# Soft-routed experts by two levels of Strassen-Winograd: weight tiles on ScalarE's queue, and the weight sums in other places

## The chip, the cores and the metric

The kernel runs on one core of one Trainium2 chip. The metric is the device time of one execution in microseconds (us). A core has TensorE (PE, matrix products), VectorE (DVE, elementwise), ScalarE (ACT, here mostly copies), GpSimd (POOL) and SyncE (SP). DMAs are issued here from the instruction streams of SyncE and GpSimd, in their order, and carried by 16 DMA engines that all share.

## The reference

```
x: (16, 512, 512) f32    router_logits: (16, 512, 8) f32    expert_weights: (8, 512, 2048) f32
probs = softmax(router_logits)
output = sum over e of probs[:, :, e:e+1] * matmul(x, expert_weights[e])     # (16, 512, 2048) f32
```

With the probabilities multiplied into x, this is one product of an 8192 x 4096 matrix (tokens by experts times hidden) with a 4096 x 2048 matrix (the weights).

## The kernel before, in words

The large product is split in two along each of its three dimensions. Tokens are taken in 16 pairs q of blocks of 256 (2q and 2q + 1). The depth is split into experts 0 to 3 and 4 to 7, the columns into 0 to 1023 and 1024 to 2047. So the weights have four blocks, B11, B12, B21 and B22 (first digit: experts, second: columns). Strassen-Winograd needs seven products of sums of blocks, P1 to P7, instead of eight. Their right sides are B11 (P1), B21 (P2), T1 = B11 - B12 (P5), T2 = B22 + T1 (P6), T3 = B22 - B12 (P7), T4 = B21 - T2 (P4) and B22 (P3).

Each right side has four sub-blocks kn = (k, n), in f16 tiles of 128 x (8 x 512), 1 MB each (k: a pair of experts, n: 512 columns). A second level of the same scheme multiplies them in seven steps, in the order 1, 5, 6, 2, 7, 3, 4. Steps 1, 2 and 3 use the raw sub-blocks (0,0), (1,0) and (1,1); steps 5, 6, 7 and 4 use sums of them ("inner sums"), made by VectorE. So each right side is seven 1 MB tiles. The pool `wpool` has 15 tiles: a right side in use is seven, and the next one is built beside it.

One step is eight matmuls (128 x 512 output) and is called a slot: 8 x 0.216 = 1.73 us. A stage runs the seven steps of one or two products in turn, so a two-product stage has 14 slots, 24.17 us. The stages:

| stages | products | starts at (us) |
|---|---|---|
| 0 to 3 | P1, two q each | 42.2 |
| 4 to 9 | P2 and P1 | 147.8 |
| 10 to 14 | P2 alone, two q each | 292.9 |
| 15 (`k5`), 16 | P5 of q = 0 and 1; P6 of q = 0 (seven slots) | 419.9 |
| 17 to 30 | P6 and P5 | 456.3 |
| 31 (`k7`) | P6 and P7 | 797.1 |
| 32 to 46 | P4 and P7 | 829.5 |
| 47 (`k3`) | P4 and P3 | 1193.1 |
| 48 to 54, 55 | P3, two q each; the last P3 (seven slots) | 1228.6 |

What surrounds the steps:

- The left side of a step is x times a probability (`times`, z tiles), with differences; VectorE makes it one stage ahead. x comes as a block of 256 tokens: either cast to f16 by GpSimd's DMA into `xs` and turned by two DMA transposes on SyncE's queue (L393, `xT<-xs`), or loaded already turned (`xT<-x`). `start_loads(stage + 2)` is issued after slot 0 of a stage, `finish_loads(stage + 2)` (the transposes) after slot 6. There are 10 x tiles.
- After a step its PSUM bank is evacuated (`post`). A product that adds to an earlier one (P2, P6, P4) does it on VectorE (`h<-ps,h`, `ps<-ps,h`), with one copy on ScalarE (L532). A product that stands alone (P1, P5, P7, P3) has five ScalarE copies (L514, L518, L521) and two VectorE additions. The addend is an `h` tile that SyncE loads one stage ahead (`h<-kept`, `h<-out_dram`); results leave as `out_dram<-h` on GpSimd's queue. There are 12 h tiles and 8 PSUM banks. The bank of step 1 is written again by step 6, three slots after step 1 ends in a two-product stage.
- `at(stage, slot, f)` runs f just before that slot in program order. Every DMA and every VectorE and ScalarE instruction of the main part is pinned to its engine's program order. `later(cost, make)` queues VectorE work; a planner (`slack`, `need`) puts it between evacuations by its estimated cost, first in, first out; 2.29 is its cost of a whole-tile sum, 0.69 of a quarter.

The weights before the change:

- `cast_block(q, kn)` casts one sub-block from f32 (two GpSimd DMAs of 512 KB). `fetch_w` loads a stored f16 tile on SyncE's queue. `kept_w` names the copy in DRAM.
- `wedge` makes half a sub-block of T3, T1 and T2 and stores them. The wedges of (0,1) run in stages 0 and 1, and with them T4 of (0,1) in stage 2 (`early_t4`); those of the other three sub-blocks run in stages 4 to 9.
- P7's inner sums are made from four whole T3 tiles in stages 10 and 11 and stored. T1 and T2 are fetched in stages 12 and 13, P5's inner sums are made in stage 14, P6's in stage 15.
- T4 of the other three sub-blocks is made in stages 17 to 20 (`t4_at`). P4's inner sums are made by quarters (two of a tile's eight chunks at a time, all four sub-blocks in one tile) in stages 21 to 26, P3's in stages 35 to 44 (`sums_by_parts`).
- `turnover(stage, place, r, raw)` brings in the seven tiles of the next right side, one in two slots, as the tiles of the old one come free: for P7 in stages 29 and 30, for P4 in 30 and 31, for P3 in 45 and 46. P3's three raw tiles are cast anew from the f32 weights.

Of the kernel before, what the change touches and what calls it, by code (L numbers as in the profile page):

```python
# [31 lines left out]
def kernel(  # L32
# [125 lines left out]

    def fetch_w(what, kn):
        t = new_w()  # L160
        sp(t, stored[what, kn])
        return t

    def inner_sums(b, t7=None):
# [579 lines left out]
    def wedge(kn, e):  # L744

        t = new_w()
        a, b = t[:, ds(0, C), :], t[:, ds(C, C), :]
        rows = ds(e * C, C)

        def casts():  # L750
            cast_w(12, kn, e, a)
            cast_w(22, kn, e, b)

        def send(what, u):
            pool(kept_w(what, kn)[:, rows, :], u)

        def t3():
            u = new_u().rearrange("p (c two) t -> p c (two t)", two=2)
            tt(u, b, a, SUB)
            send("t3", u)  # L760

        def t1():
            tt(a, b11[kn][:, rows, :], a, SUB)
            send("t1", a)

        def t2():
            if kn == (0, 1):
                tt(b11[kn][:, rows, :], b, a, ADD)
                send("t2", b11[kn][:, rows, :])
            else:  # L770
                tt(b, b, a, ADD)
                send("t2", b)
        return casts, [t3, t1, t2]

    def wedge_at(stage, slot, kn, e, then):
# [15 lines left out]
    def cast21(kn):  # L791
        b21[kn] = cast_block(21, kn)

    def early_t4():
        kn = 0, 1

        def make():
            t = new_w()
            tt(t, b21[kn], b11[kn], SUB)
            pool(kept_w("t4", kn), t)  # L800
        later(2.29, make)

    wedge_at(0, 4, (0, 1), 0, (0, 13))
    at(0, 11, lambda: cast21((0, 1)))
    wedge_at(1, 2, (0, 1), 1, (1, 11))
    at(1, 8, lambda: cast21((0, 0)))
    at(2, 2, early_t4)
    at(2, 3, lambda: cast21((1, 1)))
    at(2, 10, lambda: cast21((1, 0)))

    def sums_at(stage, slot, r, of, ps):
        def go():
# [12 lines left out]
    def fetch_at_w(stage, slot, of, what, kn):  # L825
        at(stage, slot, lambda: of.__setitem__(kn, fetch_w(what, kn)))
    ORDER = ((0, 0), (0, 1), (1, 1), (1, 0))


    def sums_in_place(part, b, r, cost):  # L830

# [7 lines left out]
        one(6, b[1, 1], b[1, 1], b[0, 0])  # L839
        one(4, b[1, 0], b[1, 0], b[1, 1])  # L840

    def whole_sums(r, b):
        sums_in_place(lambda p, o: pool(kept_w((r, p), (0, 0)), o), b, r, 2.29)

    for i, kn in enumerate(ORDER):
        fetch_at_w(10, 1 + 3 * i, t3, "t3", kn)
        fetch_at_w(12, 1 + 3 * i, t1, "t1", kn)
        fetch_at_w(13, 1 + 3 * i, t2, "t2", kn)
    at(11, 2, lambda: whole_sums(7, t3))
    last2 = k5 - 1  # L850
    sums_at(last2, 4, 5, t1, (5,))
    sums_at(last2, 6, 5, t1, (6, 7))
    sums_at(last2, 8, 5, t1, (4,))
    sums_at(k5, 3, 6, t2, (5, 6))
    sums_at(k5, 8, 6, t2, (7, 4))


    def slots_after(stage, slot, n):
# [3 lines left out]
            stage += 1  # L862
        return stage, slot

    def t4_at(stage, slot, kn):
        t = []

        def make():
            tt(t[0], t[0], t2[kn], SUB)
            pool(kept_w("t4", kn), t.pop())  # L870
        at(stage, slot, lambda: t.append(cast_block(21, kn)))
        at(*slots_after(stage, slot, 11), lambda: later(2.29, make))

    def sums_by_parts(stage, slot, every, r, load):

        for j in range(4):
            b, chunks = {}, ds(2 * j, 2)

            def begin(b=b, j=j, chunks=chunks):
                t = new_w()  # L880
                for i, kn in enumerate(ORDER):
                    b[kn] = t[:, ds(2 * i, 2), :]
                    load(b[kn], kn, j, chunks)

            def go_on(b=b, chunks=chunks):
                sums_in_place(lambda p, o: pool(kept_w((r, p), (0, 0))[:, chunks, :], o), b, r, 0.69)
            at(*slots_after(stage, slot, j * every), begin)
            at(*slots_after(stage, slot, j * every + 8), go_on)

    def cast_part(t, kn, j, chunks):  # L890
        k, n = kn
        pool(t, expert_weights[HE + 2 * k + j // 2, ds(j % 2 * 2 * P, 2 * P),
                               ds(NH + n * NB, NB)].rearrange("(c p) n -> p c n", p=P))

    for i, kn in enumerate(((0, 0), (1, 0), (1, 1))):
        t4_at(*slots_after(k5 + 2, 4, 20 * i), kn)
    sums_by_parts(*slots_after(k5 + 2, 4, 62), 20, 4,
                  lambda t, kn, j, chunks: sp(t, kept_w("t4", kn)[:, chunks, :]))
    sums_by_parts(k7 + 4, 4, 36, 3, cast_part)


    RAW = {1: (0, 0), 2: (1, 0), 3: (1, 1)}

    def turnover(stage, place, r, raw):
# [2 lines left out]

        def fetch(p):
            if p in RAW:
                right[r].w[p] = raw(RAW[p])  # L910
            else:
                right[r].w[p] = new_w()
                sp(right[r].w[p], kept_w((r, p), (0, 0)))
        at(stage - 1, 9, lambda: fetch(1))
        for i, p in enumerate(STEPS[1:]):
            at(stage, place + 2 * i + 1, lambda p=p: fetch(p))
    turnover(k7 - 1, 1, 7, lambda kn: fetch_w("t3", kn))
    turnover(k7, 0, 4, lambda kn: fetch_w("t4", kn))
    turnover(k3 - 1, 1, 3, lambda kn: cast_block(22, kn))


    finish = products[3, 15]
# [72 lines left out]
```

## Time and profile before

| | |
|---|---|
| median of 3 runs | 1416.78 us (1416.09 to 1418.22) |
| the profiled execution | 1416.24 us, of which the span from first to last instruction is 1414.4 |
| matmul spacing in an undisturbed stage | 0.216 us |
| DMA queue of GpSimd (q0, software_dynamic) | 179.87 MB, 52.7% of 16 engines |
| DMA queue of SyncE (q1, hardware_dynamic) | 159.13 MB, 36.2% |
| whole-tile sum on VectorE (`w<-w`, 128 x 4096 f16) | 2.284 us |
| quarter sum (128 x 1024 f16) | 0.684 us |
| 1 MB tile from DRAM (`w<-wd`) | 13.7 us to landing (median of 30) |
| 256 KB quarter from DRAM (`w<-wd`) | 5.6 us (median of 16) |
| cast of 512 KB, of 256 KB | 11.2 us, 7.5 us (medians) |

One execution was profiled. Durations of instructions are of that execution; a group's idle time is put down to the event that came last before it ended. "To landing" is the time from the issue of a DMA to its completion. Times in the text count from the span's start.

### The profile page before, as it was taken

The numbers are of one execution on the slowest core, as the hardware profiler recorded it, in microseconds if no ns is written. First come the engines' busy times: TensorE is split into PE (matmuls) and PEld (weight loads), VectorE is DVE, ScalarE is ACT, GpSimd is POOL, SyncE is SP. The second block draws the span as 40 slices with busy tenths as digits, with TensorE's granted clock in tenths as the row PEclk, the third lists the DMA queues.
The fourth block names the chain that finished last, engine by engine and source line by source line (L and its number), as shares of the span: only waits on it lengthen the run. The fifth ranks groups of instructions, "written<-read, shape, count | busy, mean of one in ns | idle before, by whom it ended". The sixth has DMA issues, their size and how long they took to land.

```text
span 1414.4 us, 17403 instructions
## 1 busy us (share of the span) xinstructions
PE 1377.9 (97%) x6390; PEld 624.0 (44%) x6390; DVE 1105.4 (78%) x1271; ACT 183.8 (13%) x318; POOL 383.8 (27%) x600
## 2 busy tenths in 40 slices
PE   8998999999989999999999899999999999899998
PEld 4443444444434444444444344444444444344444
DVE  4956767669679888887877688888888986798882
ACT  2221111100001111111111000000000000122221
POOL 3233333321212232222211112232332333122231
PEclk9999999999999999999999999999999999999999
DMA  9999999998987989887975898888888889988786
GB/s 196 206 254 305 250 217 280 238 379 314 370 277 211 230 244 281 267 254 238 282 216 209 323 360 231 202 230 191 240 202 223 215 215 246 228 185 183 165 154 107
DMA packets 191893, 340.10 MB, mean 240 GB/s; under 512 B 52416, under 2 KB 87488, under 8 KB 186944
## 3 DMA queue, kind: packets, MB, share of 16 engines
q0 software_dynamic: 86576, 179.87, 52.7%
q1 hardware_dynamic: 105232, 159.13, 36.2%
q8 instruction: 50, 0.82, 0.2%
q14 instruction: 35, 0.29, 0.1%
HBM read 211.85 MB, written 155.39 MB: 260 GB/s over the span
## 4 chain that ended last, share of the span: by engine, by line
PE 81%; DMA 11%; DVE 3%; issue 2%; SPq 1%; POOL 1%; ACT 0%; DVEq 0%; POOLq 0%; ACTq 0%
PE ps L127 81%; DMA h<-kept 3%; DMA w<-in_expert_weights_dram 2%; DMA xT<-xs 2%; DMA out_dram<-h 2%; DMA h<-out_dram 1%; SPq L393 1%; DVE h L107 1%; DVE z L107 1%; DMA xs<-in_x_dram 1%; DMA xT<-x 1%; DMA w<-wd 1%; POOL w L121 0%; DVE w L107 0%; POOL out_dram L121 0%
## 5 line engine op out<-in xcount | busy, mean ns | idle before, releaser
L127 PE MATMUL ps<-w,z 128*128 128x512 f16 x5416 | 1182.6, 380 | 17.8 <-DVE h L107 15.4
L127 PEld LDWEIGHTS <-z 128*128 128x128 f16 x5416 | 530.6, 98 | 659.1 <-issue 23.3
L121 POOL DMA_DIRECT2D out_dram<-h x380 | 248.6, 679 | 838.0 <-ACT h L532 433.6
L107 DVE TENSOR_TENSOR h<-ps,h 128x512 f32<-128x512 f32 x415 | 281.8, 688 | 212.2 <-PE ps L127 184.2
L107 DVE TENSOR_TENSOR z<-xT,pT 128x2048 f16<-128x2048 f16 x220 | 267.1, 1218 | 21.3 <-DMA xT<-xs 14.8
L127 PE MATMUL ps<-w,d 128*128 128x512 f16 x880 | 203.1, 384 | 11.6 <-DVE ps L107 11.6
L127 PEld LDWEIGHTS <-d 128*128 128x128 f16 x880 | 87.1, 99 | 119.0 <-issue 17.9
L107 DVE TENSOR_TENSOR z<-z,d 128x2048 f16<-128x2048 f16 x110 | 132.6, 1217 | 0.0
L521 ACT COPY h<-ps 128x512 f32<-128x512 f32 x90 | 52.8, 587 | 389.2 <-PE ps L127 353.0
L532 ACT COPY h<-ps 128x512 f32<-128x512 f32 x64 | 37.6, 587 | 501.9 <-PE ps L127 499.6
L107 DVE TENSOR_TENSOR w<-w 128x1024 f16<-128x1024 f16 (+2 forms) x72 | 96.0, 1336 | 0.5
L107 DVE TENSOR_TENSOR z<-z,u 128x2048 f16<-128x2048 f16 x64 | 78.4, 1225 | 2.2
L107 DVE TENSOR_TENSOR u<-xT,pT 128x2048 f16<-128x2048 f16 x64 | 78.0, 1219 | 0.0
L107 DVE TENSOR_TENSOR d<-z 128x1024 f16<-128x1024 f16 x110 | 75.4, 686 | 2.6 <-PE ps L127 0.5
L518 ACT COPY h<-ps 128x512 f32<-128x512 f32 x90 | 52.9, 588 | 177.4 <-PE ps L127 167.7
L107 DVE TENSOR_TENSOR ps<-ps,h 128x512 f32<-128x512 f32 (+1 forms) x66 | 45.4, 689 | 26.4 <-PE ps L127 15.5
L121 POOL DMA_DIRECT2D w<-in_expert_weights_dram x61 | 46.1, 775 | 31.3 <-PE ps L127 11.6
L107 DVE TENSOR_TENSOR h<-h 128x512 f32<-128x512 f32 (+2 forms) x69 | 45.0, 675 | 11.7 <-DMA h<-kept 9.9
L121 POOL DMA_DIRECT2D kept<-h x56 | 30.7, 550 | 56.1 <-DVE h L107 19.6
L121 POOL DMA_DIRECT2D wd<-w x56 | 31.3, 559 | 39.3 <-DVE w L107 32.2
L514 ACT COPY ps<-ps 128x512 f32<-128x512 f32 x45 | 25.7, 571 | 117.3 <-PE ps L127 116.9
L107 DVE TENSOR_TENSOR z<-z 128x2048 f16<-128x2048 f16 x32 | 39.2, 1225 | 1.1
(45 smaller groups left out, 90.4 us busy)
## 6 DMA issues: line engine op xcount, KB each, us to landing
out_dram<-h POOLq DMA_DIRECT2D x380, 256.0 KB, 6.2
pT<-p_dram SPq DMA_DIRECT2D x140, 256.0 KB, 6.2
w<-wd SPq DMA_DIRECT2D x30, 1024.0 KB, 13.7
h<-kept SPq DMA_DIRECT2D x100, 256.0 KB, 5.7
xT<-x SPq DMA_DIRECT2D x87, 256.0 KB, 5.4
w<-in_expert_weights_dram POOLq DMA_DIRECT2D x43, 512.0 KB, 11.2
h<-out_dram SPq DMA_DIRECT2D x68, 256.0 KB, 5.6
kept<-h POOLq DMA_DIRECT2D x56, 256.0 KB, 6.8
```

The lines of the kernel that those rows point to most:

```text
L107: dve(nc.vector.tensor_tensor(out=o, in0=a, in1=b, op=op))
L121: note(nc.gpsimd.dma_start(out=o, in_=i, **how))
L127: note(nc.tensor.matmul(ps, z, w, start=start, stop=stop, skip_group_check=True))
L393: note(nc.sync.dma_start_transpose(out=self.t[:, :, ds(j * P, P)], in_=self.xs[:, j, :]))
L514: act(nc.scalar.copy(self.banks["b"], x))
L518: act(nc.scalar.copy(o[tn], q if p == 5 else x))
L521: act(nc.scalar.copy(o[TN[p]], b if p == 2 else x))
L532: act(nc.scalar.copy(o[tn], b))
```

## The change

1. `fetch_w` issues its DMA from ScalarE's stream instead of SyncE's. All three turnovers now use it, and they fetch one tile in three slots instead of two.
2. The wedges of (0,1) and `early_t4` go from stages 0 to 2. The four casts for P2's sums are placed ten slots apart. The T blocks of (0,1) (called `ODD`) are made from whole tiles in stages 10 to 15, from casts of all four blocks; T1 and T2 of (0,1) stay in SBUF, T3 and T4 are stored.
3. T1 of the other sub-blocks is fetched in stage 12, T2 in stage 14. P5's inner sums are made in stages 12 and 13, P6's in 14 and 15.
4. P7's inner sums are made by quarters in stages 17 to 20, from T3 quarters loaded on ScalarE's queue.
5. P4's quarters in stages 21 to 26 cast B21, subtract T2, store T4 and then make the inner sums; `t4_at` goes.
6. P3's quarters in stages 35 to 44 also store the raw B22 in f16, and the turnover to P3 fetches those tiles instead of casting.

The diff, cut to its core:

```diff
     def fetch_w(what, kn):
         t = new_w()
-        sp(t, stored[what, kn])
+        note(nc.scalar.dma_start(out=t, in_=stored[what, kn]))
         return t
     def inner_sums(b, t7=None):
...
             send("t1", a)
         def t2():
-            if kn == (0, 1):
-                tt(b11[kn][:, rows, :], b, a, ADD)
-                send("t2", b11[kn][:, rows, :])
-            else:
-                tt(b, b, a, ADD)
-                send("t2", b)
+            tt(b, b, a, ADD)
+            send("t2", b)
         return casts, [t3, t1, t2]
     def wedge_at(stage, slot, kn, e, then):
...
     def cast21(kn):
         b21[kn] = cast_block(21, kn)
-    def early_t4():
-        kn = 0, 1
-        def make():
-            t = new_w()
-            tt(t, b21[kn], b11[kn], SUB)
-            pool(kept_w("t4", kn), t)
-        later(2.29, make)
-    wedge_at(0, 4, (0, 1), 0, (0, 13))
-    at(0, 11, lambda: cast21((0, 1)))
-    wedge_at(1, 2, (0, 1), 1, (1, 11))
-    at(1, 8, lambda: cast21((0, 0)))
-    at(2, 2, early_t4)
-    at(2, 3, lambda: cast21((1, 1)))
-    at(2, 10, lambda: cast21((1, 0)))
+    for i, kn in enumerate(((0, 0), (0, 1), (1, 1), (1, 0))):
+        at(i * 10 // 14 + (i * 10 % 14 + 2) // 14, (i * 10 + 2) % 14, lambda kn=kn: cast21(kn))
     def sums_at(stage, slot, r, of, ps):
         def go():
...
     def fetch_at_w(stage, slot, of, what, kn):
         at(stage, slot, lambda: of.__setitem__(kn, fetch_w(what, kn)))
     ORDER = ((0, 0), (0, 1), (1, 1), (1, 0))
+    ODD = 0, 1
+    made = {}
+    def cast_odd(q):
+        made[q] = cast_block(q, ODD)
+    def odd_t():
+        def make1():
+            t1[ODD] = made[11]
+            tt(t1[ODD], made[11], made[12], SUB)
+        def make3():
+            tt(made[12], made[22], made[12], SUB)
+            pool(kept_w("t3", ODD), made.pop(12))
+        def make2():
+            t2[ODD] = made[22]
+            tt(t2[ODD], made[22], t1[ODD], ADD)
+        for make in (make1, make3, make2):
+            later(2.29, make)
+    def odd_t4():
+        def make():
+            tt(made[21], made[21], t2[ODD], SUB)
+            pool(kept_w("t4", ODD), made.pop(21))
+        later(2.29, make)
     def sums_in_place(part, b, r, cost):
...
         one(6, b[1, 1], b[1, 1], b[0, 0])
         one(4, b[1, 0], b[1, 0], b[1, 1])
-    def whole_sums(r, b):
-        sums_in_place(lambda p, o: pool(kept_w((r, p), (0, 0)), o), b, r, 2.29)
-    for i, kn in enumerate(ORDER):
-        fetch_at_w(10, 1 + 3 * i, t3, "t3", kn)
-        fetch_at_w(12, 1 + 3 * i, t1, "t1", kn)
-        fetch_at_w(13, 1 + 3 * i, t2, "t2", kn)
-    at(11, 2, lambda: whole_sums(7, t3))
     last2 = k5 - 1
-    sums_at(last2, 4, 5, t1, (5,))
-    sums_at(last2, 6, 5, t1, (6, 7))
-    sums_at(last2, 8, 5, t1, (4,))
-    sums_at(k5, 3, 6, t2, (5, 6))
-    sums_at(k5, 8, 6, t2, (7, 4))
+    for stage, slot, q in ((10, 1, 12), (10, 8, 22), (11, 1, 11)):
+        at(stage, slot, lambda q=q: cast_odd(q))
+    at(11, 10, odd_t)
+    for i, kn in enumerate(((0, 0), (1, 1), (1, 0))):
+        fetch_at_w(12, 1 + 4 * i, t1, "t1", kn)
+        fetch_at_w(last2, 2 + 2 * i, t2, "t2", kn)
+    sums_at(last2 - 2, 13, 5, t1, (5, 6))
+    sums_at(last2 - 1, 6, 5, t1, (7, 4))
+    at(last2, 8, lambda: cast_odd(21))
+    sums_at(last2, 11, 6, t2, (5, 6))
+    at(k5, 4, odd_t4)
+    sums_at(k5, 5, 6, t2, (7, 4))
     def slots_after(stage, slot, n):
...
             stage += 1
         return stage, slot
-    def t4_at(stage, slot, kn):
-        t = []
-        def make():
-            tt(t[0], t[0], t2[kn], SUB)
-            pool(kept_w("t4", kn), t.pop())
-        at(stage, slot, lambda: t.append(cast_block(21, kn)))
-        at(*slots_after(stage, slot, 11), lambda: later(2.29, make))
-    def sums_by_parts(stage, slot, every, r, load):
+    def part_of(what, kn, chunks):
+        return kept_w(what, kn)[:, chunks, :]
+    def by_parts(stage, slot, every, r, load, between, when):
         for j in range(4):
             b, chunks = {}, ds(2 * j, 2)
...
                     load(b[kn], kn, j, chunks)
             def go_on(b=b, chunks=chunks):
-                sums_in_place(lambda p, o: pool(kept_w((r, p), (0, 0))[:, chunks, :], o), b, r, 0.69)
+                for kn in b:
+                    if kn != ODD:
+                        between(b[kn], kn, chunks)
+            def end(b=b, chunks=chunks):
+                sums_in_place(lambda p, o: pool(part_of((r, p), (0, 0), chunks), o), b, r, 0.69)
             at(*slots_after(stage, slot, j * every), begin)
-            at(*slots_after(stage, slot, j * every + 8), go_on)
-    def cast_part(t, kn, j, chunks):
-        k, n = kn
-        pool(t, expert_weights[HE + 2 * k + j // 2, ds(j % 2 * 2 * P, 2 * P),
-                               ds(NH + n * NB, NB)].rearrange("(c p) n -> p c n", p=P))
-    for i, kn in enumerate(((0, 0), (1, 0), (1, 1))):
-        t4_at(*slots_after(k5 + 2, 4, 20 * i), kn)
-    sums_by_parts(*slots_after(k5 + 2, 4, 62), 20, 4,
-                  lambda t, kn, j, chunks: sp(t, kept_w("t4", kn)[:, chunks, :]))
-    sums_by_parts(k7 + 4, 4, 36, 3, cast_part)
+            if between is not None:
+                at(*slots_after(stage, slot, j * every + when[0]), go_on)
+            at(*slots_after(stage, slot, j * every + when[-1]), end)
+    def cast_part(q):
+        def load(t, kn, j, chunks):
+            k, n = kn
+            pool(t, expert_weights[(q // 10 - 1) * HE + 2 * k + j // 2, ds(j % 2 * 2 * P, 2 * P),
+                                   ds((q % 10 - 1) * NH + n * NB, NB)].rearrange("(c p) n -> p c n", p=P))
+        return load
+    def load_part(what):
+        def load(t, kn, j, chunks):
+            note(nc.scalar.dma_start(out=t, in_=part_of(what, kn, chunks)))
+        return load
+    def load_p4(t, kn, j, chunks):
+        (load_part("t4") if kn == ODD else cast_part(21))(t, kn, j, chunks)
+    def less_t2(t, kn, chunks):
+        def make():
+            tt(t, t, t2[kn][:, chunks, :], SUB)
+            pool(part_of("t4", kn, chunks), t)
+        later(0.69, make)
+    def keep_raw(t, kn, chunks):
+        pool(part_of("b22", kn, chunks), t)
+    by_parts(k5 + 2, 4, 14, 7, load_part("t3"), None, (7,))
+    by_parts(*slots_after(k5 + 2, 4, 58), 21, 4, load_p4, less_t2, (7, 13))
+    by_parts(k7 + 4, 4, 36, 3, cast_part(22), keep_raw, (9, 16))
     RAW = {1: (0, 0), 2: (1, 0), 3: (1, 1)}
...
         def fetch(p):
             if p in RAW:
-                right[r].w[p] = raw(RAW[p])
+                right[r].w[p] = fetch_w(raw, RAW[p])
             else:
-                right[r].w[p] = new_w()
-                sp(right[r].w[p], kept_w((r, p), (0, 0)))
+                right[r].w[p] = fetch_w((r, p), (0, 0))
         at(stage - 1, 9, lambda: fetch(1))
         for i, p in enumerate(STEPS[1:]):
-            at(stage, place + 2 * i + 1, lambda p=p: fetch(p))
-    turnover(k7 - 1, 1, 7, lambda kn: fetch_w("t3", kn))
-    turnover(k7, 0, 4, lambda kn: fetch_w("t4", kn))
-    turnover(k3 - 1, 1, 3, lambda kn: cast_block(22, kn))
+            at(*slots_after(stage, place + 1, 3 * i), lambda p=p: fetch(p))
+    turnover(k7 - 1, 1, 7, "t3")
+    turnover(k7, 0, 4, "t4")
+    turnover(k3 - 1, 1, 3, "b22")
     finish = products[3, 15]
```

## The prediction

> **What bounds the kernel now.** I read the page first, for the busiest engine; then the windows view by stage, for where that engine loses time; then the waits of TensorE, the timeline of VectorE in those stages, and the queue's own waits of SyncE with the DMA view, for what was late.
>
> ```profile
> span 1414.4 us, 17403 instructions
> PE 1377.9 (97%) x6390; PEld 624.0 (44%) x6390; DVE 1105.4 (78%) x1271; ACT 183.8 (13%) x318; POOL 383.8 (27%) x600
> ```
>
> TensorE is the bound, so only its idle time can be won. The windows view (columns: window, its length, busy time of each engine, granted clock, DMA share, GB/s) places it. The third row is an undisturbed two-product stage, 24.16 us; the others are stages 1, 2, 14, 17, 31, 32 and 47.
>
> ```profile
> 66.34:91.32 24.98, 24.33 (x113) 10.97 (x112) 13.85 (x14) 5.84 (x10) 10.05 (x16) 1.00 1.15 271
> 91.33:123.63 32.30, 25.99 (x113) 11.35 (x112) 20.27 (x20) 5.84 (x10) 10.27 (x17) 0.95 1.16 279
> 123.64:147.80 24.16, 24.16 (x113) 10.97 (x112) 17.68 (x16) 5.84 (x10) 6.66 (x12) 1.00 0.97 267
> 389.54:419.92 30.38, 26.01 (x113) 11.39 (x112) 21.51 (x23) 1.17 (x2) 3.26 (x7) 0.94 0.89 301
> 456.29:482.82 26.53, 24.34 (x113) 10.88 (x112) 22.73 (x28) 2.92 (x5) 6.62 (x11) 1.00 1.10 263
> 797.08:829.47 32.39, 26.68 (x113) 11.52 (x112) 22.00 (x27) 1.76 (x3) 4.32 (x9) 0.89 0.95 371
> 829.48:854.43 24.95, 24.32 (x113) 10.91 (x112) 20.34 (x24) 1.17 (x2) 5.40 (x9) 1.00 1.01 379
> 1193.07:1228.61 35.54, 26.99 (x113) 11.53 (x112) 21.74 (x24) 2.92 (x5) 7.10 (x9) 0.90 0.98 259
> ```
>
> The excess over 24.16 is 0.8 + 8.1 + 6.2 + 2.4 + 8.2 + 0.8 + 11.4 = 37.9 us; the waits view adds 0.8 us near the end: 38.7 us in all. Where the granted clock is under 1, matmuls ran at half speed after the stop, so a long stop costs more than its length (stage 2: 0.05 of 32.3 = 1.6 us more).
>
> Each long stop is VectorE late with a PSUM evacuation. The timeline (start, length, what, idle time before with its releaser) shows what held VectorE in stages 2, 14, 31 and 47:
>
> ```profile
> 112.67 1.22 DVE L107 TENSOR_TENSOR z<-xT,pT 128x2048 f16<-128x2048 f16 x1 [6.57 <-PE ps L127]
> ...
> 115.74 2.28 DVE L107 TENSOR_TENSOR w<-w 128x4096 f16<-128x4096 f16 x1
> 117.94 2.48 DVE L107 TENSOR_TENSOR h<-ps,h 128x512 f32<-128x512 f32 x4
> ```
>
> ```profile
> 400.23 0.70 DVE L107 TENSOR_TENSOR ps<-ps,h 128x512 f32<-128x512 f32 x1 [8.66 <-DMA h<-kept]
> ```
>
> ```profile
> 806.16 1.90 DVE L107 TENSOR_TENSOR h<-h 128x512 f32<-128x512 f32 x3 [9.92 <-DMA h<-kept]
> ```
>
> ```profile
> 1199.17 0.69 DVE L107 TENSOR_TENSOR h<-ps,h 128x512 f32<-128x512 f32 x1 [6.93 <-DMA h<-out_dram]
> ...
> 1215.02 0.69 DVE L107 TENSOR_TENSOR h<-ps,h 128x512 f32<-128x512 f32 x1 [7.56 <-DMA out_dram<-h]
> ```
>
> The first row names TensorE, but the last transpose into that xT landed at 112.48, the moment of release. So the losses come from DMAs that landed late, in stages full of weight traffic, plus one weight sum of 2.28 us in front of four evacuations.
>
> **The change, part by part.**
>
> *T blocks of (0,1) leave stages 0 to 2.* Removed there: four casts of 512 KB, six stores of 512 KB, one of 1 MB, and on VectorE 6 x 1.22 + 2.28 = 9.6 us; the four casts for P2's sums stay. The 2.28 us is the very row in front of the evacuations at 117.94. The transposes took 15.0 us (median) in stages 1 and 2, against 7.9 us in stages 5 to 8, which have one cast block and three half-MB stores a stage, no more than stages 1 and 2 keep. The last one, issued at 95.2, would land near 103 instead of 112.5, before VectorE asks at 106. I leave 1.5 us of the 9.0; bounds 0 and 6 (if transposes stay at 15 us, only the sum is gone).
>
> *They come back in stages 10 to 15:* three casts of 1 MB in stages 10 and 11 and one in 14, 3 x 2.28 + 2.28 us on VectorE, two stores. The fetch of four t3 tiles and the whole P7 sums leave 10 and 11, and t1 and t2 shrink from eight fetches to six. VectorE is busy 15.6 of 24.17 us in stage 10 (no weight sums), so 8.5 us a stage is free. From late in stage 11 to the end of 14 the T blocks (6.9), P5's sums (9.1) and half of P6's (4.6) make 20.6 us against 3.3 x 8.5 = 28. Before, all of P5's sums sat in stage 14.
>
> *Stage 14.* What was late there is h<-kept, issued at 389.7 for a slot that began at 379.2, because SyncE was held in four transposes from 376.7 to 389.0, between weight fetches of 12.4 us each. After, no weight fetch is issued in stage 13. Two transposes alone take 2.5 us of issue at 428.2, so four take 5 and the loads go out near 382; even at 10 us they land as they are asked for (391.5). I leave 0.5 of 6.2; bounds 0 and 5.
>
> *Stage 17.* TensorE waits 2.2 us there for a z that the planner makes behind an evacuation; nothing in stage 16 changes: 2.4 stays.
>
> *Turnovers to P7 and P4 (stages 30 to 32).* In stage 30 the small loads took 16.1 us (h<-kept) and 17.0 (h<-out_dram) behind 1 MB weight tiles in SyncE's queue, while out_dram<-h, on GpSimd's queue in the same window, took 8.0. With weights on ScalarE's queue I take 8 for the loads: issued at 783.4 to 790.0 they land by 798, and VectorE's wait of 9.92 ends 8 us sooner. Then the weights may be late instead. Thirteen tiles, 13.6 MB, are needed between slot 2 of stage 30 (776) and slot 12 of stage 32 (842 if nothing stops). Beside them runs the base traffic, 199 GB/s in stages 33 and 34: 13.1 MB in 66 us. At the 371 to 379 GB/s of stages 31 and 32, 26.7 MB take 71 us: 5 us late, less what is loaded ahead. I leave 3.5 of 9.0; bounds 0 and 9.
>
> *Turnover to P3 (46, 47).* Six casts of 512 KB leave GpSimd's queue. There out_dram<-h took 10.2 us (median; the one that freed the h at 1215 took 21.5), against 5.2 in stages 33 and 34; h<-out_dram took 11.5 behind four weight fetches. Now six fetches of 1 MB from 1172 on, one in 5.2 us, are 202 GB/s beside 199: slightly over the rate above, but the last tile has 17 us to land (ten slots) where 13.7 is the median. I leave 2.5 of 11.4; bounds 0 and 8. The three b22 tiles cost twelve more quarter stores in stages 35 to 44, where TensorE never waits.
>
> *Quarters in stages 17 to 27 and 35 to 44.* P7's sums: 16 x 0.68 = 10.9 us instead of 9.1; P4's twelve subtractions: 8.2 instead of 6.9. VectorE is busy about 20 us a stage there, and a quarter adds 2.7 to 4.8 in one to one and a half stages: hidden. A cast quarter lands in 7.5 us and is used after seven slots (12.1 us).
>
> *ScalarE's stream.* 27 tile fetches and 20 quarter loads at SyncE's 0.32 us are 15 us on an engine that idles 87%. But ScalarE works in order, and behind a waiting fetch stand the PSUM copies (L514, L518, L521). A copy of a two-product stage has three slots, 5.2 us, less its own 0.59: 4.6 us of slack. SyncE's waits show how long such a fetch may stand:
>
> ```profile
> SPq L118 <- DVE z L107: 448.1, 52, 23.5
> ...
> SPq L118 <- DMA w<-wd: 45.0, 19, 4.0
> ```
>
> The second kind (2.4 us on average) is the nearer one: a fetch waiting for an earlier DMA. It fits under 4.6. For this and for waits in stages that lose nothing today I add 1.0; bounds 0 (a gain is excluded: those stages lose nothing) and 8.
>
> **Sum.** Left: 1.5 + 0.5 + 2.4 + 3.5 + 2.5 + 0.8 + 1.0 = 12.2 of 38.7, a gain of 26.5 us. The profiled execution took 1416.2 us (span 1414.4 and 1.8 around it): 1389.7, and 1390.2 against the median of 1416.8, 0.5 above it. I say 1390.
>
> **Rivals.**
>
> *The loads stay late (0.20).* If what slowed them is the full set of DMA engines and not the order in one queue, a new queue wins nothing: stages 31 and 32 keep 9.0, 14 and 47 about half, 3 and 6; the gain is 7.5 + 3.2 + 5.4 - 1.0 = 15 us: 1402. For it: DMA shares of 0.95 to 1.16 in these stages. Against it: the 8.0 us beside 16.1 in one window. The Trainium skill says it outright (DMA: Bandwidth & Descriptors, "Issuing engines are not separate DMA queues"): DMAs of all issuing engines run on the same 16 engines and interleave, so that another issuer saves only the issue time; by that alone the move would be worth nothing and the time would be this rival's. The same page ("Queues, rings and completion order") has each engine take turns between the queues, which the 8.0 beside 16.1 agrees with.
>
> *New waits in the stages that took the work (0.12).* GpSimd's stores stand behind 1 MB casts in stages 10 and 11 as they did in 46 (10.2 us), h tiles return late, and a quarter's subtraction meets a cast that has not landed. Two stops of 4 to 5 us with their half-speed matmuls: 10 us more than forecast, 1400. Against it: stages 5 to 8 carry a cast block each and lose nothing.
>
> *ScalarE stuck (0.18), slower.* A fetch waits as SyncE's loads wait for a free x tile: 8.6 us on average (448.1 / 52), 23.5 at most. Each such wait ahead of a copy stops TensorE for 8.6 - 4.6 = 4.0 us, 5.6 with the half-speed matmuls. It turns the sign from five of the 27 fetches on (26.5 / 5.6); with eight the time is 1390 + 45 = 1435. For it: SyncE issues late in all three turnovers. Against it: fetches stand one slot or more after the last reader of a tile, and ScalarE issues none of the x loads.
>
> **Chances and range.** Forecast 0.50, loads late 0.20, new waits 0.12, ScalarE stuck 0.18. 0.2% (2.8 us) is about what a measurement here can tell from no change. The first three are faster; of the last, 0.02 is a near balance and 0.16 slower; faster 0.82. The range starts where all bounds are at zero, 1416.8 - 38.7 + 3.2 = 1381, and reaches past the second and third case to 1408 (six more than 1402, for their own spread), leaving the stuck case out.
>
> **What would show it.** Right: windows of stages 2, 14 and 47 near 24 to 27 us, 31 near 27, 17 still 26.5; h<-kept near 8 us in stage 30; no ACT copy waiting on a w<-wd. Wrong: ScalarE's copies late in stages 31, 46 and 47 with TensorE waiting for ACT (stuck), or h loads still at 16 us in stage 30 (late).

## The result

The changed kernel takes 1395.30 us (median of 4 runs, 1390.09 to 1396.55); beside it the kernel before took 1416.43 (4 runs, 1415.44 to 1418.22). The ratio is 0.9842, 95% interval 0.9814 to 0.9870. The forecast was 1390, so the direction and most of the size came out, with 5 us missing. The profiled execution of after took 1396.55 us, its slowest; that of before took 1416.24. In a later comparison one execution of the kernel before took 5199.72 us, a disturbed run that is left out of the ratio.

One correction first. The section on the kernel says that a product P7 stands alone and has five copies on ScalarE. It does not: it adds to an earlier product, is evacuated by VectorE, and has one copy (L532) on ScalarE. Only P1, P5 and P3 stand alone. So in stages 32 to 46 (P4 and P7), as in stages 10 to 14 (P2 alone), ScalarE has two copies a stage and, beside the DMAs it issues, nothing else. This matters below.

### The profile page after: what moved, and what is told of

The parts are those of the page before. It is cut to its first block, busy times and chain, and to the rows that moved or that the text cites. A ratio compares the mean times of both kernels' runs of the same rounds, so it can differ in the third digit from the quotient of the medians.

```text
span 1394.9 us, 17466 instructions
## 1 busy us (share of the span) xinstructions
PE 1373.0 (98%) x6390; PEld 621.7 (45%) x6390; DVE 1106.1 (79%) x1289; ACT 183.0 (13%) x318; POOL 400.8 (29%) x632
## 4 chain that ended last, share of the span: by engine, by line
PE 84%; DMA 6%; issue 5%; DVE 3%; POOL 2%; ACT 0%; SPq 0%; DVEq 0%; POOLq 0%; ACTq 0%
PE ps L127 84%; DMA out_dram<-h 2%; DMA wd<-w 1%; DMA h<-out_dram 1%; DVE z L107 1%; DVE h L107 1%; POOL out_dram L121 1%; DVE w L107 1%; DMA w<-in_expert_weights_dram 1%; POOL w L121 0%; DMA h<-kept 0%; POOL wd L121 0%; DVE ps L107 0%; POOL kept L121 0%; ACT h L326 0%
## 5 line engine op out<-in xcount | busy, mean ns | idle before, releaser
L107 DVE TENSOR_TENSOR w<-w 128x1024 f16<-128x1024 f16 (+2 forms) x92 | 100.8, 1102 | 7.9 <-DMA out_dram<-h 7.3
L532 ACT COPY h<-ps 128x512 f32<-128x512 f32 x64 | 37.5, 586 | 496.6 <-PE ps L127 478.7
L121 POOL DMA_DIRECT2D w<-in_expert_weights_dram x65 | 48.9, 793 | 51.6 <-DMA wd<-w 37.0
L121 POOL DMA_DIRECT2D wd<-w x86 | 48.3, 584 | 41.4 <-DVE w L107 36.9
L514 ACT COPY ps<-ps 128x512 f32<-128x512 f32 x45 | 25.7, 571 | 111.3 <-PE ps L127 110.9
## 6 DMA issues: line engine op xcount, KB each, us to landing
w<-in_expert_weights_dram POOLq DMA_DIRECT2D x35, 512.0 KB, 11.2
```

The costliest lines, as they stand in the source:

```text
L107: dve(nc.vector.tensor_tensor(out=o, in0=a, in1=b, op=op))
L121: note(nc.gpsimd.dma_start(out=o, in_=i, **how))
L514: act(nc.scalar.copy(self.banks["b"], x))
L532: act(nc.scalar.copy(o[tn], b))
```

## The profile after

From the page of the changed kernel: TensorE's busy time fell by 5 us (fewer half-speed matmuls), GpSimd's rose by 17, and a queue q10 is new: ScalarE's.

```profile
span 1394.9 us, 17466 instructions
PE 1373.0 (98%) x6390; PEld 621.7 (45%) x6390; DVE 1106.1 (79%) x1289; ACT 183.0 (13%) x318; POOL 400.8 (29%) x632
...
q10 hardware_dynamic: 6768, 33.56, 6.9%
```

The windows view of the changed kernel, with the columns as before: window, its length, busy time of PE, PEld, DVE, ACT and POOL, granted clock, DMA share, GB/s. The rows are stages 1, 2, 12, 14, 17, 26, 31, 32 and 47.

```profile
65.98:90.15 24.17, 24.17 (x113) 10.94 (x112) 12.48 (x14) 5.83 (x10) 8.68 (x14) 1.00 1.13 236
90.15:114.32 24.17, 24.17 (x113) 10.93 (x112) 11.09 (x13) 5.82 (x10) 6.59 (x11) 1.00 1.20 237
331.89:361.86 29.97, 26.17 (x113) 11.36 (x112) 24.98 (x27) 1.18 (x2) 6.47 (x12) 0.94 0.88 291
386.04:410.20 24.16, 24.16 (x113) 10.94 (x112) 20.29 (x23) 1.17 (x2) 5.88 (x11) 1.00 1.07 346
446.57:473.09 26.52, 24.33 (x113) 10.85 (x112) 23.94 (x30) 2.92 (x5) 7.20 (x13) 1.00 0.94 278
667.52:694.36 26.84, 24.32 (x113) 10.94 (x112) 22.14 (x29) 3.34 (x6) 11.06 (x20) 1.00 0.95 269
791.80:815.96 24.16, 24.16 (x113) 10.94 (x112) 21.31 (x26) 1.76 (x3) 4.30 (x9) 1.00 1.03 398
815.97:840.13 24.16, 24.16 (x113) 10.94 (x112) 20.44 (x24) 1.17 (x2) 5.35 (x9) 1.00 1.04 377
1178.57:1208.99 30.42, 26.02 (x113) 11.33 (x112) 21.29 (x23) 2.91 (x5) 5.22 (x7) 0.94 0.81 219
```

Stages 1, 2, 14, 31 and 32, which lost 24.1 us before, now take the 24.17 us of an undisturbed stage. Stage 17 is unchanged, 47 is half mended. Stage 12 lost nothing before and loses 5.8 us now; stages 25 to 27 lose 1.0, 2.7 and 0.7. The losses by stage here and below are a stage's length, measured from matmul to matmul, less 24.17. Over stages 0 to 54 they sum to 19.0 us after and to 38.2 before: a difference of 19.3, and the spans differ by 19.5.

In stages 1 and 2 the loss is gone, but the transposes are hardly faster. The DMA view of both stages, before and then after (count, median us to landing), and VectorE's row in stage 2 of the changed kernel:

```profile
xT<-xs SPq DMA_TRANSPOSE x8, 15.0
```

```profile
xT<-xs SPq DMA_TRANSPOSE x7, 14.2
```

```profile
105.55 1.22 DVE L107 TENSOR_TENSOR z<-xT,pT 128x2048 f16<-128x2048 f16 x1 [3.42 <-DMA xT<-xs]
```

The last transpose of stage 2 was issued at 89.83, 0.3 us before the stage began, and landed at 105.36, 15.5 us later. Before the change it was issued at 95.24, 3.9 us after the stage began, took 17.2, and a weight sum of 2.28 us stood behind it.

The waits of TensorE in the changed kernel (engine, line, waited for: us in total, times, longest) show the same in short. The four waits of the first row are in stages 12, 25, 27 and 47 (3.2, 0.7, 0.4 and 4.4 us), the second is in stage 26, the third in 17:

```profile
PE ps L127 <- DVE ps L107: 8.7, 4, 4.4
PE ps L127 <- ACT ps L514: 2.5, 1, 2.5
PE ps L127 <- DVE z L107: 2.2, 1, 2.2
```

No row has TensorE waiting for a weight tile from ScalarE's queue. What is late now, read from the timeline of the changed kernel (start, length, what, idle time before with its releaser), VectorE's rows in stages 12 and 47 first, then ScalarE's fetches before each of them, and SyncE's load of stage 46:

```profile
333.17 2.29 DVE L107 TENSOR_TENSOR w<-w 128x4096 f16<-128x4096 f16 x1 [7.29 <-DMA out_dram<-h]
335.38 1.28 DVE L107 TENSOR_TENSOR h<-ps,h 128x512 f32<-128x512 f32 x2
```

```profile
1187.56 0.69 DVE L107 TENSOR_TENSOR h<-ps,h 128x512 f32<-128x512 f32 x1 [9.82 <-DMA h<-out_dram]
```

```profile
321.73 0.88 ACTq L161 DMA_DIRECT2D w<-wd  x2
```

```profile
1168.41 0.59 ACT L532 COPY h<-ps 128x512 f32<-128x512 f32 x1 [1.14 <-PE ps L127]
1168.47 3.72 ACTq L161 DMA_DIRECT2D w<-wd  x3
```

```profile
1171.00 0.57 SPq L118 DMA_DIRECT2D h<-out_dram  x1
```

*Stage 12.* The sum at 333.17 is the first of the three T sums of (0,1). The row names a store, but the sum doesn't read it. It reads the cast of B11(0,1), whose second half was issued on GpSimd's queue at 311.86 and landed at 333.05, 21.2 us later. Two evacuations stand behind the sum (335.38), and TensorE behind them. Beside that cast ran the first two T1 fetches of 1 MB. They were meant for slots 1 and 5 of stage 12, 333.6 and 340.5; ScalarE issued them at 321.73 and 322.28, 12 and 18 us early, since after its copy at 321.73 it had none to wait for until slot 6 of stage 12.

*Stage 47.* The load of an h tile went out on SyncE at 1171.00, behind an x load that had stood until 1169.8 for a free x tile, and that block's probabilities. It landed at 1187.44, 16.4 us later. At 1168.47, 1168.84 and 1171.86 ScalarE had issued three weight fetches of 1 MB within 3.4 us. At one fetch in three slots they should be 5.2 us apart. The first went out in its slot (slot 8 of stage 46, at 1168.2). The other two belong to slot 11 and to slot 0 of stage 47, at 1173.4 and 1178.6, and went out 4.6 and 6.7 us early: behind the copy at 1168.41 ScalarE again had none to wait for.

*Stage 26.* Two rows of ScalarE's timeline, with the fetch in its instruction queue ahead of them:

```profile
677.27 0.33 ACTq L909 DMA_DIRECT2D w<-wd  x1
677.71 0.58 ACT L521 COPY h<-ps 128x512 f32<-128x512 f32 x1 [19.91 <-DMA wd<-w]
678.19 0.59 ACT L514 COPY ps<-ps 128x512 f32<-128x512 f32 x1
```

The load of a P4 quarter waits for a free weight tile, which comes free when the sums of the quarter before have been stored (`wd<-w`). In this stretch P5 and P6 hold 14 of the 15 tiles, so there is one. The copy L514 stands behind the load, and TensorE waits 2.5 us for it. That is the rival "ScalarE stuck", once, and by a quarter load instead of a turnover's fetch. GpSimd's queue waits for the same tile, and in stages 25 and 27 VectorE waits 5.5 and 4.9 us for `h<-kept`. For stage 27 the timelines give the steps between. GpSimd sent its three quarter casts at 677.68, after 6.9 us of waiting, and the cast of an x block behind them at 680.40; it landed at 688.12. SyncE's transposes wait for that cast, went out at 688.14, and the load of h behind them was issued at 693.13 and landed at 698.49; VectorE went on at 698.58.

The small loads in stage 30, in the turnover to P7, were the point of the new queue. The DMA view of stage 30 (tiles, queue, operation, count, KB each, median us to landing), before and then after:

```profile
h<-kept SPq DMA_DIRECT2D x3, 256.0 KB, 16.1
```

```profile
w<-wd ACTq DMA_DIRECT2D x5, 1024.0 KB, 8.7
h<-kept SPq DMA_DIRECT2D x3, 256.0 KB, 7.0
h<-out_dram SPq DMA_DIRECT2D x3, 256.0 KB, 7.3
```

## The experiments

Ratios are to the kernel before on the same chip, with 95% intervals. Losses are of the profiled execution of each kernel.

### 1. The queue alone (queue_alone)

The kernel before with nothing but the new queue for its stored weight tiles:

```diff
-        sp(t, stored[what, kn])
+        note(nc.scalar.dma_start(out=t, in_=stored[what, kn]))
...
-                sp(right[r].w[p], kept_w((r, p), (0, 0)))
+                note(nc.scalar.dma_start(out=right[r].w[p], in_=kept_w((r, p), (0, 0))))
```

> The kernel before, with all weight tiles fetched from ScalarE's stream and nothing else changed (turnovers still one tile in two slots, T blocks of (0,1) still early, P3's raw tiles still cast). Theory 'order in one queue': loads of h stood behind 1 MB tiles in SyncE's queue; h<-kept in stage 30 falls from 16.1 to about 8 us, stages 31 and 32 lose under 2 us instead of 9.0, stage 14 under 2 instead of 6.2; stages 2 and 47 keep about 8 and 8 to 11. Time near 1402. Rival 'the DMA engines are full': h<-kept stays near 16 us and stages 31 and 32 keep 6 to 9; time 1412 to 1417. Rival 'ScalarE stuck': TensorE waits for ScalarE's copies, time above 1417.

Measured: 1407.64 us (1405.77 to 1409.78) beside 1417.43, ratio 0.9935 (0.9916 to 0.9954). The windows of stages 14, 31 and 47 in this kernel:

```profile
389.58:420.30 30.72, 27.42 (x113) 11.61 (x112) 22.51 (x24) 1.17 (x2) 4.85 (x9) 0.89 0.84 289
799.15:827.90 28.75, 25.97 (x113) 11.31 (x112) 21.91 (x27) 1.76 (x3) 4.09 (x9) 0.94 1.02 399
1190.67:1220.48 29.81, 26.00 (x113) 11.32 (x112) 20.76 (x23) 2.92 (x5) 7.09 (x9) 0.94 0.98 233
```

The queue alone halves the losses of stages 31 and 32 (9.0 to 4.6) and of 47 (11.4 to 5.6), and leaves stage 14 at 6.5 and stage 2 at 8.4. So what mended stage 14 in the changed kernel is that the fetches no longer run in stage 13, not the queue they are on. `h<-kept` in stage 30 took 10.6 us (median), between the 16.1 of before and the 7.0 of after. So the expectation of the queue's theory, under 2 us for stages 31 and 32 and for stage 14, missed, and the time of 1407.64 lies between its 1402 and the 1412 of the rival.

### 2. All but the queue (all_but_queue)

The changed kernel with the tile fetches and quarter loads on SyncE again:

```diff
-        note(nc.scalar.dma_start(out=t, in_=stored[what, kn]))
+        sp(t, stored[what, kn])
...
-            note(nc.scalar.dma_start(out=t, in_=part_of(what, kn, chunks)))
+            sp(t, part_of(what, kn, chunks))
```

> The kernel after, with all weight tiles and quarters fetched on SyncE's queue again. Theory 'order in one queue': h loads of stage 30 back at 12 us or more, stages 31 and 32 lose 5 to 9 us again (0 after), stage 47 8 or more (6.2 after); the waits of TensorE for ScalarE in stage 26 go (2.7). Time 1400 to 1408. Rival 'spreading and less traffic did it': stages 31 and 32 stay at 0 to 1, time 1390 to 1396.

Measured: 1412.42 us (1407.80 to 1418.39), ratio 0.9971 (0.9949 to 0.9993). Stages 1, 2, 12 and 14 lose nothing, stage 27 loses 5.1, 31 loses 10.1, 47 loses 14.3. In the waits of TensorE of this kernel stands what the changed kernel does not have:

```profile
PE ps L127 <- DMA w<-wd: 15.1, 2, 12.5
```

Slots three apart on SyncE are worth nothing: stage 31 keeps its loss, `h<-kept` took 12.8 us, and now a weight tile comes 12.5 us late in stage 47 because it stands behind the x loads. But the trace shows that this is not a slower pace in fact. In stage 30 SyncE, held until 772.5, sent three of the fetches from 773.0 to 775.7. What a pace that is kept would be worth in SyncE's own queue was not tried. The time is also longer than the 1400 to 1408 expected. That stage 12 loses nothing here says that its stop belongs to the new queue. And the moved work (1, 2, 14) needs no new queue.

### 3. Two slots instead of three (two_slots)

The changed kernel with the turnovers' fetches in every second slot, as before:

```diff
-            at(*slots_after(stage, place + 1, 3 * i), lambda p=p: fetch(p))
+            at(stage, place + 2 * i + 1, lambda p=p: fetch(p))
```

> The kernel after, with the turnovers at one tile in two slots as before (the queue stays ScalarE's). If the separate queue is what matters, stages 31 and 32 lose 0 to 2 us and the time is within 3 us of the kernel after. If the spreading over three slots matters, the h loads of stage 30 take 12 us or more, stages 31, 32 lose 3 to 9, and the time is 1398 to 1404.

Measured: 1401.20 us (1400.56 to 1402.18), ratio 0.9890 (0.9874 to 0.9906). Stage 31 loses 5.5 us (0 in the changed kernel), 47 loses 4.0, 12 loses 6.2, 25 to 27 lose 4.6. `h<-kept` in stage 30 took 11.4 us. The issues in the trace show why. In both kernels SyncE sends five small loads in stage 30, from 777.2 to 779.5 in the changed kernel and from 778.6 to 782.0 here. In the changed kernel no fetch goes out between 774.7 and 781.6, and the five have landed by 786.5. Here fetches go out at 776.2, 779.7, 783.1 and 786.6, and the fifth load lands at 800.1. With experiments 1 and 2 there are four cases for stages 31 and 32: neither the queue nor the wider slots leaves 9.0, the wider slots alone (sent in a burst by SyncE) 10.5, the queue alone 4.6 or 5.5, both together 0.

### 4. T4 of (0,1) made later (t4_later)

The kernel before with its one early sum, and the store of its result, twelve slots later:

```diff
-    at(2, 2, early_t4)
+    at(3, 0, early_t4)
```

> The kernel before, with the sum of early_t4 (2.28 us of VectorE) queued at the start of stage 3 instead of in stage 2; all DMAs of the T blocks stay. If the late x tile and the sum add up in front of the evacuations, stage 2 loses about 8.1 - 2.3 = 5.8 us or, with fewer half-speed matmuls, 4 to 5; the x tile still lands near 112 us. Time 1412 to 1415. If the DMA traffic alone counts, stage 2 keeps 8 us and the time stays at 1416.

Measured: 1413.35 us (1411.20 to 1418.92), ratio 0.9978 (0.9965 to 0.9991). Stage 2 loses 4.5 instead of 8.1, stage 3 loses 0.4; the others are within 0.8 us of before. VectorE's rows in stage 2:

```profile
110.95 1.23 DVE L107 TENSOR_TENSOR z<-xT,pT 128x2048 f16<-128x2048 f16 x1 [4.98 <-DMA xT<-xs]
...
114.02 2.51 DVE L107 TENSOR_TENSOR h<-ps,h 128x512 f32<-128x512 f32 x4
```

Counted from the stage's start the four evacuations begin 2.9 us earlier than before. The sum accounts for 2.2 of that, and 0.7 is a transpose that landed sooner in this execution. So the sum in front of the evacuations, with its half-speed matmuls, made somewhat less than half of that stage's loss (at most 3.6 of 8.1 us). With the sum gone, 4.5 us stay, in which VectorE waits for the late transpose.

### 5 to 8. One repair for each new loss, and all three

Each is an edit of the changed kernel. t1_later fetches T1 in slots 8 to 10 of stage 12, so ScalarE's two copies of that stage, from slot 6 on, have to come first:

```diff
-        fetch_at_w(12, 1 + 4 * i, t1, "t1", kn)
+        fetch_at_w(12, 8 + i, t1, "t1", kn)
```

> The kernel after, with the three T1 fetches of stage 12 at slots 8, 9 and 10 instead of 1, 5 and 9, so that ScalarE's two copies of stage 12 stand in front of them. Theory 'ScalarE ran ahead': with no copies between stage 11's slot 7 and stage 12's slot 6 two fetches went out 10 us early, at 321.7, beside the cast of B11(0,1), which landed at 333.0 and held VectorE 7.3 us. Then the cast lands by 328, stage 12 loses under 1.5 us instead of 5.8, and the time is 4 to 6 us under the kernel after. Rival 'the cast is late by its own queue' (its second half was issued at 311.9 behind six stores): it still lands at 331 or later and stage 12 keeps 4 to 6 us.

p4_28 starts a P4 quarter every 28 slots:

```diff
-    by_parts(*slots_after(k5 + 2, 4, 58), 21, 4, load_p4, less_t2, (7, 13))
+    by_parts(*slots_after(k5 + 2, 4, 58), 28, 4, load_p4, less_t2, (7, 13))
```

> The kernel after, with P4's quarters every 28 slots (two stages) instead of 21. Theory 'the quarter's tile': in stages 24 to 27 the loads on ScalarE and GpSimd waited for the one free tile, because the second and fourth quarter's sums stood behind the next stage's left sides; at 28 every quarter's sums end before the next begins. Then ScalarE never waits for a wd<-w store, TensorE does not wait for ScalarE, stages 25 to 27 lose under 1 us instead of 4.4. Time 3 to 5 us under the kernel after. Rival 'the stages are simply full' (DMA share 0.91 to 0.95): the stops move to other stages of 21 to 28 and the time changes by under 1.5 us.

h_first issues the last h load of the last P7 four slots sooner, ahead of the x loads that SyncE waits with:

```diff
-        for slot, tn in zip((7, 9, 11, 17), INNER):
+        for slot, tn in zip((7, 9, 11, 17 if q < 15 else 13), INNER):
```

> The kernel after, with the last h<-out_dram of the last P7 (q = 15) issued at slot 13 of stage 45 instead of slot 3 of stage 46, ahead of the x loads of stage 48. Theory 'place in SyncE's order': that load was issued at 1171.0 because it stood behind x loads that wait for x tiles, then met three weight fetches sent at once by ScalarE and took 16.4 us. Issued near 1155 it lands before 1165; stage 47 loses under 2 us instead of 6.2 and the time is 4 to 6 us under the kernel after. Rival 'the burst of three weight tiles is what stops stage 47': another load or store is late there and 3 to 6 us stay.

all_three has the three edits together.

> The kernel after with the three edits together: T1 fetches at slots 8 to 10 of stage 12, P4's quarters every 28 slots, the last h<-out_dram of q = 15 ahead of stage 48's x loads. If the three stops have separate causes their gains add: 5.8 + 4.4 + 6.2 less 2 to 4 that stay, 12 to 14 us under the kernel after, 1380 to 1384. If one DMA limit is behind all of them, a stop that is taken away comes back elsewhere and the gain is under 8 us.

| kernel | us (range) | ratio to before (interval) | lost in stage 12 | 25 to 27 | 47 |
|---|---|---|---|---|---|
| after | 1395.30 (1390.09 to 1396.55) | 0.9842 (0.9814 to 0.9870) | 5.8 | 4.4 | 6.2 |
| t1_later | 1390.12 (1388.60 to 1391.68) | 0.9808 (0.9786 to 0.9829) | 0 | 2.5 | 7.5 |
| p4_28 | 1393.27 (1391.24 to 1395.08) | 0.9829 (0.9806 to 0.9852) | 6.8 | 0 | 6.9 |
| h_first | 1387.70 (1386.54 to 1392.24) | 0.9798 (0.9769 to 0.9828) | 4.3 | 1.1 | 0 |
| all_three | 1383.51 (1380.37 to 1384.84) | 0.9756 (0.9735 to 0.9777) | 0 | 0 | 0 |

Beside these four kernels the kernel before took 1417.27 us. Each edit takes away the loss it aims at, and the other two stay, though not at the same size (stages 25 to 27 lose 2.5 in t1_later and 1.1 in h_first). By time alone the first three can't be told from the changed kernel, as their intervals overlap with its own; all_three can. In t1_later the cast landed at 328.58, 17.2 us after its issue instead of 21.2, and the row of that sum names it as what it waited for:

```profile
328.70 2.29 DVE L107 TENSOR_TENSOR w<-w 128x4096 f16<-128x4096 f16 x1 [2.62 <-DMA w<-in_expert_weights_dram]
```

In h_first ScalarE still sends three fetches within 3.4 us (1165.85 to 1169.24), and stage 47 loses nothing: the burst alone does not stop TensorE. p4_28 brought 2.0 us in the median where its stages lost 4.4, less than the 3 to 5 expected: stages 25 to 27 vary (1.1 to 4.5 us among the kernels that share that part), and in its own profile stage 12 lost a microsecond more. In p4_28 ScalarE waited for a store of weights once, 2.8 us, instead of 5.4 and 19.9.

### 9. P3's raw tiles cast again (casts_again)

all_three, with the three raw tiles of P3 cast from f32 on GpSimd's queue as the kernel before had them (the copies stored for them stay, unread):

```diff
-                right[r].w[p] = fetch_w(raw, RAW[p])
+                right[r].w[p] = cast_block(22, RAW[p]) if r == 3 else fetch_w(raw, RAW[p])
```

> The kernel all_three, with P3's three raw tiles cast anew from the f32 weights by GpSimd at the turnover to P3 (as before the change) instead of fetched; slots and everything else as in all_three. If the casts in GpSimd's queue were what held the stores and stopped stage 47 before the change, out_dram<-h of stages 46 and 47 goes to 10 us or more, stage 47 loses 5 to 10 us (0 in all_three) and the time is 5 to 10 us over all_three. If the place of the h and weight loads in SyncE's queue was the cause, stage 47 loses under 2 us and the time is within 2 us of all_three.

Measured: 1389.29 us (1388.65 to 1390.34) beside 1418.48, ratio 0.9802 (0.9788 to 0.9816); its interval lies above that of all_three. Stage 46 loses 7.3 us, and VectorE's row there names a store on GpSimd's queue:

```profile
1159.34 0.69 DVE L107 TENSOR_TENSOR h<-ps,h 128x512 f32<-128x512 f32 x1 [7.25 <-DMA out_dram<-h]
```

The five stores that GpSimd issued right behind the first two casts, from 1143.21 to 1147.72, took 16.0 to 18.3 us, and the first of them landed at 1159.22, just before that row; in all_three no store of stages 45 and 46 took more than 14.1. So the casts do hold h tiles back, by the mechanism the prediction named. But here the stop is in stage 46, and stage 47, where the prediction and the expectation have it, loses nothing. By the medians the casts cost 5.8 us; in the profiled execution stage 17 also lost 1.7 us more, which the edit does not touch.

### 10. Stage 17 as well (four)

all_three, with the first left sides of both products of stage 17 queued ahead of the rest, for the one wait that the change had left alone:

```diff
+            first = stages[stage] if stage == 17 else ()
+            for p in first:
+                p.left.queue_make(0)
             for p in stages[stage]:
-                p.left.queue_make(0)
+                if p not in first:
+                    p.left.queue_make(0)
```

> The kernel all_three, with stage 17's left sides queued so that the first z of both products comes ahead of the rest. The 2.35 us of stage 17, the same in every run, are the z of P5's first step, which the planner makes behind an evacuation after slot 0. If it is only the order, stage 17 loses under 0.5 us and the time falls by 2 us against all_three. If VectorE has no room in stage 16 (11.2 us busy of 12.1), another z is late by as much and the time stays.

Measured: 1378.63 us (1377.99 to 1380.90), ratio 0.9726 (0.9712 to 0.9739). Its own run of before is 1418.48; the interval just touches that of all_three. TensorE's waits of this kernel have no row for z any more:

```profile
PE ps L127 <- DMA w<-in_x_dram: 1.8, 2, 1.1
PE ps L127 <- DVE h L107: 1.3, 3, 0.8
PE every L89 <- DVE h L86: 1.3, 1, 1.3
```

In stages 0 to 54 it loses 2.1 us in all (1.2 in stage 22, 0.5 in 47, 0.4 in 2). It is the fastest kernel run here, 17 us under the changed one; TensorE is busy for 1369.3 of its 1379.2 us.

## Why the prediction was right, and where it was not

*The bound and the way of counting held.* Only TensorE's idle time could be won, and it was: the stages' losses fell by 19.3 us and the span by 19.5.

*T blocks of (0,1).* Left 0 of 9.0, forecast 1.5. Both causes were right: experiment 4 has the sum at somewhat less than half of stage 2's loss and the late transpose behind the rest. The step that was to mend the transposes failed: they were to take 7.9 us instead of 15.0, and took 14.2 (median), the last one 15.5. The prediction's own bound for that case was 6 us left. That nothing was left is luck as far as the prediction goes: the last transpose was issued 4.2 us earlier in its stage, which the prediction did not count on, and no sum stood behind it. Why it was issued earlier was not tried.

*Stage 14.* Left 0 of 6.2, forecast 0.5. The reason given holds: no weight fetch in stage 13, and the loads of `h<-kept` that were issued at 389.7, as stage 14 began, go out from 378.1 on, 7.9 us before it begins. Experiment 1 excludes the new queue as the reason, since with it alone the stage keeps 6.5.

*Stage 17.* 2.4 forecast, 2.4 measured, and experiment 10 shows that it was the order in which z tiles are made.

*Stages 31 and 32.* Left 0, forecast 3.5. That the small loads would take 8 us was right (7.0 and 7.3). The 3.5 were for weights coming late, and TensorE never waited for one. What the prediction did not see is that the queue would not do it alone: experiments 1 and 3 show that it needs the pace as well, since with a fetch every other slot the loads took 10.6 to 11.4 us even in a queue of their own.

*Stage 47.* The step by which six casts leave GpSimd's queue, the h load no longer stands behind fetches and 2.5 us are left was mis-sized: 6.2 were left. That casts in GpSimd's queue hold h tiles back holds (experiment 9, in stage 46). The other half took the new queue as enough for the h load. It still took 16.4 us, behind x loads in its own queue and beside three fetches sent in a burst. The kernel h_first, which only issues the load sooner, takes the loss away.

*Quarters.* P7's and P3's were hidden, as forecast: stages 18 to 24 and 35 to 44 lose nothing. P4's, from stage 25 on, were not.

*ScalarE's stream and new waits.* This is the term that failed most: 1.0 forecast, with 8 as its upper bound, and 10.2 measured (5.8 in stage 12, 4.4 in 25 to 27). The step asked only how long a waiting fetch holds the copies behind it. It took the slot in program order for the time of issue. ScalarE, with two copies a stage, runs ahead of its slots as soon as it has none to wait for (12 and 18 us in stage 12, 4.6 and 6.7 in stage 46). The rule it needed is the other way round: what holds the fetch back, rather than what the fetch holds up. Stages 25 to 27 are the rival "ScalarE stuck" in small: one wait of TensorE of 2.5 us where 5.6 each was its price, and none of them by the 27 tile fetches.

*The rival "new waits".* It had 0.12, and it is what came, nearly at its price: 10 us more in the stages that took the work, against 10.2 in stages 12 and 25 to 27. A sum did meet a cast that had not landed (stage 12), and h tiles did come late where GpSimd's queue was held (stages 25 and 27). What held them was another thing than the rival said: fetches sent early by ScalarE in the first place, and a quarter's load waiting for the one free weight tile in the second. Stages 10 and 11, where the rival had the stores behind casts, lose nothing.

*The errors cancel in part.* Of the places to be mended, stages 1, 2, 14, 31 and 32 kept 5.5 us less than forecast and 47 kept 3.7 more; the new losses are 9.2 more. That makes 7.4 us, and the profiled execution lies 6.9 above the 1389.7 forecast for it. So the time came nearer to the forecast than its terms did.

*The rival "the loads stay late".* Its price was 1402 and experiment 1 shows how far it holds. The new queue alone is worth 10 us, so it is not worth nothing; but it halves the losses of stages 31, 32 and 47 and no more. The Trainium skill (DMA: Bandwidth & Descriptors, "Issuing engines are not separate DMA queues") would have only the issue time saved. The trace disagrees for a small load behind large ones: `h<-kept` fell from 16.1 us to 10.6, counted from issue to landing, so with no issue time in it. It agrees in that the transfers still share the DMA engines: with a gap between the fetches of the same queue, the same load took 7.0.

## What to carry to other kernels

A queue of its own for large transfers keeps small loads from standing behind them, but here the two still shared the DMA engines, so the large ones had to be paced too: the queue alone left half the loss of stages 31 and 32, wider slots in the old queue all of it. A slot in program order paces a DMA only if its engine has something to wait for in that slot: put the issue behind an instruction that waits for the right moment, and look in the trace at when it was really issued. And before a load that waits for a tile goes on an engine that evacuates PSUM, work out when that tile comes free, with the stores that free it.

## What the runs showed of the hardware that was not expected

- DMA transposes took 14.2 us (median, issue to landing) in stages 1 and 2 when the eight weight casts in these stages had become five and their seven weight stores had gone, and 15.0 before: that traffic made little of their length. What made it stays open.
- A load of 256 KB took 16.4 us in a queue that held only two loads as small ahead of it, beside three 1 MB fetches on another queue; in stage 30 such loads took 7.0 (median) where no fetch was issued between 774.7 and 781.6, though three followed within 3.7 us.
- Half of a cast of 1 MB, 512 KB on GpSimd's queue, took 21.2 us beside two 1 MB fetches and 17.2 without them; the median of such casts before was 11.2.
- The same stop of 2.35 us in stage 17 cost 2.36 us in eight of the profiled executions and 4.05 in three (queue_alone, h_first and casts_again), where eight matmuls after it ran at half speed: 8 x 0.21 us more. What decides between the two stays open.
